# A two-layer diffusion backbone step on one core: the program records its instructions and orders each engine's queue itself, with the modulation products ranked last

## The chip, the core and the metric

The kernel runs on one core of one Trainium2 chip. Five engines of that core have a queue of their own and work through it strictly in order: TensorE (PE, matmuls; PEld are its weight loads), VectorE (DVE), ScalarE (ACT), GpSimd (POOL) and SyncE (SP), which here only issues the transfers from and to HBM. They meet through semaphores: an instruction that has to wait for another engine holds up all that is queued behind it on its own engine. The metric is the device time of one execution in microseconds (us), the median of several; lower is better. "Granted clock" is the share of TensorE's full clock that the chip granted in a stretch.

## The reference, cut to what matters

One inference step of a backbone of two layers, width 1024, on 128 context tokens and 512 latent tokens (640 columns in all), float32:

```
for each layer:
  shift, scale, gate (x2) = SiLU(cond) @ w_mod + b_mod      # cond = c (latent) or c_ctx (context)
  h = RMSNorm(x) * (1 + scale_a) + shift_a
  p = h @ w_in                                              # feeds all four mixers
  o_ssd = bidirectional Mamba-2 scan, 8 heads               # conv, softplus(dt), chunks of 128
  o_ret = bidirectional retention, 4 heads
  o_att = grouped-query attention, 8 heads, rotary
  o_mla = latent attention, 8 heads (two low-rank projections)
  g     = sigmoid(h @ w_merge + b_merge)                    # 1024 -> 4 x 1024
  x += gate_a * RMSNorm((sum_b g_b * (o_b @ w_br_b)) @ w_out)
  h = RMSNorm(x) * (1 + scale_f) + shift_f
  u = conv3(h @ w_ffn_up)                                   # 1024 -> 2 x 2816
  x += gate_f * RMSNorm((silu(u_gate) * u_up) @ w_ffn_down)
```

It returns both token groups and the final scan states and caches of the context.

## The kernel before

**Products.** Activations lie with features on the partitions, 640 columns of tokens. Each float32 operand is split in two parts, and each product is three matmuls: `wh*ah`, `wh*al`, `wl*ah`. Weights come as 128x512 blocks: SP loads `wr` (L333), ACT rounds it to `wh` (L305), POOL takes the difference `wl` (L308), and PE runs 128x128x320 matmuls over it (`mm`, L321; sums in `lin`). Activations come back through DVE and ACT: `tt` (L308), `stt` (L311), `tsc` (L316 and L318), `act` (L305). Other names in the rows: `st` and `pv` are PSUM tiles of scores, sums and attention values, `K` and `Q` keys, queries and conv inputs, `X` the residual or the accumulated merge, `g` gates, `ah` and `al` the two parts of the input of a product, `m` scratch, `la` the log decay of the scan.

**Stages.** `mixer` runs for each layer: `w_in` blocks with the SSD mixer, retention, attention, `merge` 0 to 2 (gates of a branch, its projection and the sum into `X`), the latent attention, and `merge_out` (merge 3, `w_out`, the two norms). `ffn` follows, with `up(f)` for 22 blocks and `down` in groups. The heavy products are dealt out between the heads of the mixers, so that PE has work while a chain of DVE and ACT works on a head.

**Modulation.** Layer 0's modulation is computed at the start on PE (`first`). Layer 1's, and the part of layer 0's that its second half needs, are computed while layer 0 runs (`mod_units`): a block of `w_mod` is loaded as 128x512, and DVE multiplies it with SiLU(cond) and sums along the row (L584, `wj<-K,silc` or `wj<-g,silc`, 320 of them, all in layer 0: each followed by a read of the accumulator). `fill(n)` takes n of them: 8 ahead of each of the 8 output blocks of a merge, 2 ahead of each block of merge 3, 5 after each `up(f)`, 2 ahead of each block of a `down`, and what is left with `fill(1000)`. Their weight tiles share the tags of the merge's `K` tiles (12) or of the FFN's `g` tiles (5).

**What sets the order.** The Tile framework orders each engine's queue, by the order in which the program is written and by hand-made edges: `tc.issue_after(x)` puts the instructions inside it behind x. `behind()` puts the matmuls of a head behind the PE instruction written last, `go_on` does so for the steps of the norms and scans that are dealt out between matmuls, `rowsum` and `first` for theirs, and `fill` puts the products behind `self.last`, the last DVE operation of an FFN block.

```
    def behind(self, on=True):
        return self.tc.issue_after(self.pe) if on else nullcontext()
```

## Time and profile before

| | |
|---|---|
| time, median of 3 runs | 3076.99 us (3075.81 to 3079.99) |
| the profiled execution | 3081.01 us, span of its trace 3079.2 us |
| busy: PE, PEld | 2911.7 us (95%), 2723.7 us (88%) |
| busy: DVE, ACT, POOL | 2019.1 us (66%), 1385.2 us (45%), 1148.1 us (37%) |
| granted clock of TensorE, mean | 0.975 |
| HBM traffic | 326.37 MB, 106 GB/s over the span |

Layer 0 runs from about 20 to 1586 us and layer 1 from there to the end. Busy time on PE is the time in which a matmul was in its pipeline; it says where PE stood still, not how well it was used. A timeline row gives the start, the length (of several in a row, from the first to the last), the engine, the line, the operation with output and inputs, the count and, in square brackets, the idle time ahead of it on its engine and what ended that. A windows row gives for one stretch (its bounds and its length) the busy time with the number of instructions of PE, PEld, DVE, ACT and POOL, then the granted clock, the share of the DMA engines and GB/s.

### The profile page before, as it was taken

The numbers are of one execution on the slowest core, as the hardware profiler recorded it, in microseconds if no ns is written. First come the engines' busy times: TensorE is split into PE (matmuls) and PEld (weight loads), VectorE is DVE, ScalarE is ACT, GpSimd is POOL, SyncE is SP. The second block draws the span as 40 slices with busy tenths as digits, with TensorE's granted clock in tenths as the row PEclk, the third lists the DMA queues.
The fourth block names the chain that finished last, engine by engine and source line by source line (L and its number), as shares of the span: only waits on it lengthen the run. The fifth ranks groups of instructions, "written<-read, shape, count | busy, mean of one in ns | idle before, by whom it ended". The sixth has DMA issues, their size and how long they took to land. (4 is left out here: it accounts for less than half of the span.)

```text
span 3079.2 us, 50917 instructions
## 1 busy us (share of the span) xinstructions
PE 2911.7 (95%) x18638; PEld 2723.7 (88%) x18638; DVE 2019.1 (66%) x3758; ACT 1385.2 (45%) x3013; POOL 1148.1 (37%) x889
## 2 busy tenths in 40 slices
PE   8999999999988899999988999999999999999998
PEld 4888898898888889899988899988988988999997
DVE  3678727637996588888776872177277455655556
ACT  3435246646634533332355353366477445433333
POOL 1223341131146653443463233411411566433334
PEclk9999999999999899999999999999999999999999
DMA  6215421143365434443243133211332433222223
GB/s 207 72 50 177 152 85 39 55 133 120 104 212 165 130 99 131 137 127 117 89 135 99 54 126 93 84 41 50 123 112 92 135 119 115 92 76 76 76 74 107
DMA packets 193418, 329.71 MB, mean 107 GB/s; under 512 B 20880, under 2 KB 54288, under 8 KB 193168
## 3 DMA queue, kind: packets, MB, share of 16 engines
q1 hardware_dynamic: 193168, 326.46, 34.1%
q8 instruction: 146, 2.39, 0.3%
q14 instruction: 104, 0.85, 0.1%
HBM read 293.41 MB, written 32.96 MB: 106 GB/s over the span
## 5 line engine op out<-in xcount | busy, mean ns | idle before, releaser
L308 POOL TENSOR_TENSOR wl<-wr,wh 128x512 fp32r<-128x512 f32 (+2 forms) x790 | 1076.5, 1366 | 1811.9 <-PE lin L321 1196.4
L321 PE MATMUL lin<-ah,wh 128*128 128x320 f32 (+1 forms) x3776 | 1173.4, 317 | 16.6 <-ACT ah L305 4.8
L321 PE MATMUL lin<-al,wh 128*128 128x320 f32 (+1 forms) x3776 | 1164.8, 315 | 12.5 <-DVE al L308 9.9
L321 PE MATMUL lin<-ah,wl 128*128 128x320 f32 x3744 | 949.2, 314 | 5.7 <-POOL wl L308 5.1
L305 ACT ACTIVATE wh<-wr 128x512 fp32r<-128x512 f32 (+2 forms) x796 | 486.7, 616 | 923.6 <-PE lin L321 491.7
L321 PEld LDWEIGHTS lin<-ah,wh 128*128 128x128 f32 (+1 forms) x3776 | 720.9, 191 | 32.6 <-ACT ah L305 6.6
L321 PEld LDWEIGHTS lin<-al,wh 128*128 128x128 f32 (+1 forms) x3776 | 719.8, 191 | 28.5 <-DVE al L308 13.8
L321 PEld LDWEIGHTS lin<-ah,wl 128*128 128x128 f32 x3744 | 656.5, 191 | 17.5 <-POOL wl L308 9.5
L308 DVE TENSOR_TENSOR m<-m,m 128x512 fp32r<-128x512 f32 (+6 forms) x393 | 310.1, 795 | 231.2 <-ACT m L305 225.5
L321 PE MATMUL lin<-K,wh 128*128 128x320 f32 (+1 forms) x1472 | 298.9, 316 | 16.6 <-ACT K L305 7.2
L305 ACT ACTIVATE m<-st 128x512 fp32r<-128x512 f32 (+2 forms) x480 | 223.3, 523 | 124.2 <-PE st L321 99.7
L321 PEld LDWEIGHTS lin<-K,wh 128*128 128x128 f32 x1472 | 240.7, 191 | 21.4 <-ACT K L305 7.8
L321 PE MATMUL lin<-O,wh 128*128 128x320 f32 x1024 | 215.7, 315 | 12.4 <-ACT O L305 4.6
L321 PE MATMUL lin<-K,wl 128*128 128x320 f32 (+1 forms) x736 | 187.5, 316 | 4.7 <-POOL wl L308 4.6
L321 PE MATMUL pv<-m,K 128*128 128x512 f32 (+2 forms) x832 | 184.1, 343 | 2.7 <-DVE m L308 2.5
L321 PEld LDWEIGHTS lin<-O,wh 128*128 128x128 f32 x1024 | 168.7, 191 | 18.6 <-DVE O L308 5.1
L584 DVE SCALAR_TENSOR_TENSOR wj<-g,silc 128x512 bf16<-128x512 f32 x160 | 148.1, 925 | 2.0
L584 DVE SCALAR_TENSOR_TENSOR wj<-K,silc 128x512 bf16<-128x512 f32 x160 | 139.3, 871 | 4.2 <-DMA K<-in_wmod 1.6
L321 PEld LDWEIGHTS pv<-m,K 128*64 128x64 f32 (+1 forms) x832 | 117.5, 160 | 27.1 <-DVE m L308 6.9
L305 ACT ACTIVATE m<-m 128x641 f32<-128x641 f32 (+4 forms) x116 | 82.4, 714 | 129.3 <-DVE m L311 120.5
L321 PEld LDWEIGHTS lin<-K,wl 128*128 128x128 f32 x736 | 129.6, 191 | 7.6 <-POOL wl L308 7.6
L1182 DVE TENSOR_REDUCE nm<-st 128x1 f32<-128x320 f32 (+1 forms) x288 | 123.9, 461 | 17.5 <-PE st L321 16.3
(209 smaller groups left out, 3360.6 us busy)
## 6 DMA issues: line engine op xcount, KB each, us to landing
wr<-in_wup SPq DMA_DIRECT2D x196, 256.0 KB, 2.7
wr<-in_wmg SPq DMA_DIRECT2D x160, 256.0 KB, 2.7
wr<-in_win SPq DMA_DIRECT2D x142, 256.0 KB, 2.6
K<-in_wmod SPq DMA_DIRECT2D x112, 256.0 KB, 3.9
wr<-in_wdn SPq DMA_DIRECT2D x94, 256.0 KB, 2.7
wr<-in_wbr SPq DMA_DIRECT2D x80, 256.0 KB, 2.7
g<-in_wmod SPq DMA_DIRECT2D x80, 256.0 KB, 2.9
wr<-in_wout SPq DMA_DIRECT2D x64, 256.0 KB, 2.8
```

The lines of the kernel that those rows point to most:

```text
L305: self.nc.scalar.activation(out, in_, func, **kw)
L308: return (eng or self.nc.vector).tensor_tensor(out, a, b, op).ins
L321: self.pe = self.nc.tensor.matmul(out, lhsT, rhs, start=start, stop=stop).ins
L584: self.nc.vector.scalar_tensor_tensor(junk[:, :512], w[:, :512], 0.5, si, ALU.mult, ALU.mult, accum_out=acc)
L1182: self.nc.vector.tensor_reduce(t[:, j * 8 + i : j * 8 + i + 1], p[:, :w], AX.X, ALU.max, negate=True)
```

## The change

The program no longer issues instructions while it is written. Every call goes to a `Recorder`, which notes the operation with the regions that it reads and writes. At the end `depend()` finds the dependences, `order()` plays all five queues against a table of durations, and `emit()` issues the instructions in the order of the starts so found, with the framework's own ordering switched off. In `order()` an engine that is free takes the operation with the lowest rank among those that could start; the rank is the place in the program, and an operation hands its rank on to what it needs. Buffers are part of it: an operation that needs a new tile can't start before one is free. `issue_after` becomes empty, so that none of the hand-made edges is left. The products of `mod_units` get a rank 4000 later (`BEHIND`), may not start before the last matmul written ahead of their `fill` (`gate`), and their weights get a tag of their own with 2 buffers (`wm`). The buffers of `g` go from 5 to 4 and those of `wh` from 4 to 3. The computation and the number of instructions on each engine stay the same.

```
-GB = 5
+GB = 4
-WR, WB, WL = 4, 4, 3
+WR, WB, WL = 4, 3, 3
+BEHIND = 4000
+LAT = {"tensor": 260.0, "vector": 90.0, "scalar": 90.0, "gpsimd": 110.0, "sync": 60.0}
+SLACK = 250.0
+DMA_ISSUE, DMA_NS, DMA_RATE = 400.0, 1900.0, 330.0
+class Recorder:
+    def add(self, eng, name, args, kw):
...
+        o.prio, o.gate = o.i + self.bias, self.gate
+    def cost(self, o):
...
+        if o.eng == "tensor":
...
+                return max(110.0, 10 + n * 0.428)
...
+        if o.eng == "vector":
+            if o.name == "reciprocal":
+                return 60 + 6.4 * n
+            if o.name in ("tensor_scalar", "memset"):
+                return 170 + 0.76 * n
+            if o.name == "scalar_tensor_tensor":
+                return 200 + 1.08 * n + (90 if "accum_out" in o.kw else 0)
+            return 180 + 1.06 * n
+        if o.eng == "scalar":
+            return 200 + 0.86 * n + (210 if "accum_out" in o.kw else 0)
+        if o.eng == "gpsimd":
...
+            return 260 + 2.12 * n
...
+    def depend(self):
...
+            if o.gate is not None:
+                o.preds.add(o.gate)
...
+        for o in reversed(self.ops):
+            for q in o.preds:
+                q.prio = min(q.prio, o.prio)
+    def order(self):
...
+            p, i = heappop(avail[e])
+            o = self.ops[i]
+            b = blocked(o, t) if o.new else None
...
+            for q in o.succs:
+                lat = 0.0 if q.eng == e and e != "sync" else LAT[e] + (SLACK if q.eng == "tensor" else 0.0)
+                q.ready = max(q.ready, o.end + lat)
...
+        done.sort(key=lambda o: o.start)
+    def emit(self):
+        done = self.order()
...
+        with self.tc.manual_schedule():
+            for o in done:
+                f = getattr(getattr(nc, o.eng), o.name)
+                f(*[_plain(v) for v in o.args], **{k: _plain(v) for k, v in o.kw.items()})
 class Net:
-        self.tc, self.nc, self.A = tc, tc.nc, A
+        self.rec = self.nc = Recorder(tc)
+    @staticmethod
+    def issue_after(ins):
+        return nullcontext()
     def mod_units(self, l, blocks, halves, tile, pool=()):
-                    w = self.modw(F32)
+                    self.rec.bias = BEHIND
+                    w = self.sbt(512, "wm", 2)
     def fill(self, n):
-        with self.tc.issue_after(self.last) if self.last is not None else nullcontext():
-            for _ in range(n):
+        self.rec.gate = self.pe
+        for _ in range(n):
...
+        self.rec.gate = None
 def build(tc, A, dbg=None):
-        Net(ctx, tc, A, dbg).run()
+        net = Net(ctx, tc, A, dbg)
+        net.run()
+        net.rec.emit()
-    with _tile.TileContext(nc, auto_bufs=True) as tc:
+    with _tile.TileContext(nc) as tc:
```

Three places show how instructions move. The first number of a row is its place in the engine's queue; a name carries the number that the program gave the tile, the same in both kernels, and a running number behind it. In the changed kernel the line is that of the recorder's call (L581).

VectorE at the end of merge 2 in layer 0, before: `X` takes the gated branch, `al` is the input of the `w_out` product made from it.

```order
1087 L308 TENSOR_TENSOR X_538_2794<-g_2457_10830,X_538_2794 128x320
1088 L584 SCALAR_TENSOR_TENSOR wj_2456_10828,modr_2154_9493<-K_2454_10824,silc_2176_9542 128x512
1089 L308 TENSOR_TENSOR X_539_2795<-g_2472_10896,X_539_2795 128x320
1090 L584 SCALAR_TENSOR_TENSOR wj_2470_10892,modr_2154_9493<-K_2469_10890,silc_2174_9537 128x512
1091 L584 SCALAR_TENSOR_TENSOR wj_2471_10894,modr_2154_9493<-K_2469_10890,silc_2176_9542 128x512
1092 L311 SCALAR_TENSOR_TENSOR g_2487_10962<-g_2487_10962,lin_2495_11001 128x320
1093 L584 SCALAR_TENSOR_TENSOR wj_2485_10958,modr_2154_9493<-K_2484_10956,silc_2174_9537 128x512
1094 L308 TENSOR_TENSOR X_540_2796<-g_2487_10962,X_540_2796 128x320
1095 L584 SCALAR_TENSOR_TENSOR wj_2486_10960,modr_2154_9493<-K_2484_10956,silc_2176_9542 128x512
1096 L308 TENSOR_TENSOR al0_26_98<-X_534_2790,ah0_18_90 128x320
```

And VectorE at the same place in the changed kernel:

```order
1063 L581 SCALAR_TENSOR_TENSOR g_2487_11007<-g_2487_11007,lin_2495_10994 128x320
1064 L581 TENSOR_TENSOR X_540_3975<-g_2487_11007,X_540_3975 128x320
1065 L581 TENSOR_TENSOR al0_26_294<-X_534_3051,ah0_18_290 128x320
1066 L581 TENSOR_TENSOR al1_27_307<-X_535_3271,ah1_19_301 128x320
1067 L581 TENSOR_TENSOR al2_28_322<-X_536_3471,ah2_20_318 128x320
1068 L581 TENSOR_TENSOR al3_29_343<-X_537_3606,ah3_21_331 128x320
1069 L581 TENSOR_TENSOR al4_30_354<-X_538_3727,ah4_22_351 128x320
1070 L581 TENSOR_TENSOR al5_31_375<-X_539_3851,ah5_23_361 128x320
1071 L581 TENSOR_TENSOR al6_32_412<-X_540_3975,ah6_24_404 128x320
1072 L581 SCALAR_TENSOR_TENSOR wj_2283_11085,modr_2154_10334<-wm_2282_10527,silc_2174_10285 128x512
1073 L581 SCALAR_TENSOR_TENSOR g_2502_11071<-g_2502_11071,lin_2510_11064 128x320
```

No product stands any more between `X_538` and `al6`; two stand around the last `X`, and the other products of this merge follow in a row behind `al7`.

TensorE at the first scores of attention in layer 1 (`K_4510` the keys, `Q_4519` the queries that DVE makes), before:

```order
11080 L321 MATMUL lin_4897_22677<-ah3_3589_16618,wl_4900_22680 128x320
11081 L321 MATMUL lin_4896_22676<-ah4_3590_16619,wh_4902_22709 128x320
11082 L321 MATMUL st_4522_21520<-K_4510_21476,Q_4519_21514 128x320
11083 L321 MATMUL st_4523_21523<-K_4510_21476,Q_4519_21514 128x320
11084 L321 MATMUL st_4524_21526<-K_4510_21476,Q_4519_21514 128x320
11085 L321 MATMUL lin_4896_22676<-al4_3598_16627,wh_4902_22709 128x320
```

In the changed kernel TensorE has at these scores:

```order
11121 L581 MATMUL lin_4896_21670<-ah7_3593_17415,wl_4903_21638 128x320
11122 L581 MATMUL lin_4897_21673<-ah7_3593_17415,wl_4903_21638 128x320
11123 L581 MATMUL lin_4905_21752<-O_4870_21297,wh_4908_21688 128x320
11124 L581 MATMUL st_4522_21756<-K_4510_20476,Q_4519_21727 128x320
11125 L581 MATMUL st_4523_21758<-K_4510_20476,Q_4519_21727 128x320
11126 L581 MATMUL st_4524_21760<-K_4510_20476,Q_4519_21727 128x320
```

The scores move behind the rest of the gate block `lin_4896`, `lin_4897` (4 of its 8 steps) and the first matmul of the next one: 24 matmuls more stand ahead of them.

VectorE at the start of the SSD scan in layer 1 (`m_3882` the softplus of dt on 128x80, 128x641 the convolution taps), before:

```order
1835 L311 SCALAR_TENSOR_TENSOR m_3909_18064<-K_3759_17325,hc_3583_16606,m_3909_18064 128x641
1836 L311 SCALAR_TENSOR_TENSOR m_3882_17964<-m_3882_17964 128x80
1837 L311 SCALAR_TENSOR_TENSOR g_4036_18578<-g_4036_18578,lin_4037_18579 128x320
1838 L311 SCALAR_TENSOR_TENSOR m_3882_17964<-m_3882_17964 128x80
1839 L311 SCALAR_TENSOR_TENSOR g_4036_18578<-g_4036_18578,lin_4038_18580 128x320
1840 L311 SCALAR_TENSOR_TENSOR dt_3881_17963<-m_3882_17964 128x80
1841 L318 TENSOR_SCALAR m_3912_18072<-K_3760_17326,hc_3583_16606 128x641
1842 L311 SCALAR_TENSOR_TENSOR la_3884_17984<-dt_3881_17963,ea_3883_17982 128x80
```

In the changed kernel VectorE has ahead of the same `la`:

```order
1803 L581 SCALAR_TENSOR_TENSOR O_3893_18049<-m_3894_18041,m_3892_18020 128x641
1804 L581 TENSOR_SCALAR m_3882_18047<-m_3882_18047 128x80
1805 L581 RECIPROCAL m_3882_18047<-m_3882_18047 128x80
1806 L581 TENSOR_TENSOR m_3882_18047<-m_3882_18047 128x80 x2
1807 L581 TENSOR_SCALAR m_3882_18047<-m_3882_18047 128x80
1808 L581 SCALAR_TENSOR_TENSOR m_3882_18047<-m_3882_18047 128x80 x8
1809 L581 TENSOR_SCALAR m_3882_18047<-dtx_3880_18043 128x80
1810 L581 SCALAR_TENSOR_TENSOR dt_3881_18111<-m_3882_18047 128x80
1811 L581 SCALAR_TENSOR_TENSOR la_3884_18115<-dt_3881_18111,ea_3883_16703 128x80
```

The convolution taps that stood between the steps of the softplus are gone from it, most of them to places ahead of it. On TensorE the cumulative sums that read `la` move from place 9175 to 9121 of the queue.

## Rows read from the trace of the kernel before

**Rows 1.** The page's first part: busy time, share of the span, instructions

```profile
PE 2911.7 (95%) x18638; PEld 2723.7 (88%) x18638; DVE 2019.1 (66%) x3758; ACT 1385.2 (45%) x3013; POOL 1148.1 (37%) x889
```

**Rows 2.** Windows (columns as told above): five stretches of layer 0, then of layer 1

```profile
135.60:466.80 331.20, 312.97 (x2098) 292.92 (x2097) 220.55 (x508) 128.41 (x298) 112.69 (x86) 0.99 0.36 112
474.50:681.00 206.50, 204.68 (x1272) 185.44 (x1272) 121.55 (x199) 119.42 (x255) 50.57 (x41) 1.00 0.22 68
681.00:883.30 202.30, 187.18 (x1113) 164.55 (x1111) 173.83 (x321) 121.56 (x252) 42.93 (x41) 0.98 0.44 139
883.30:1159.30 276.00, 240.83 (x1483) 232.14 (x1483) 201.96 (x361) 122.72 (x255) 158.93 (x113) 0.91 0.46 143
1159.30:1586.30 427.00, 408.51 (x2688) 400.16 (x2688) 360.67 (x673) 145.04 (x335) 184.66 (x133) 0.98 0.40 123
1694.40:2012.50 318.10, 309.42 (x2087) 289.40 (x2086) 161.62 (x375) 127.01 (x296) 109.89 (x86) 0.99 0.29 89
2020.20:2226.90 206.70, 204.62 (x1272) 185.40 (x1272) 120.12 (x198) 119.10 (x253) 52.49 (x41) 1.00 0.22 68
2226.90:2418.80 191.90, 185.28 (x1113) 164.49 (x1113) 135.33 (x216) 123.49 (x254) 44.16 (x42) 0.98 0.36 113
2418.80:2667.10 248.30, 230.13 (x1485) 224.40 (x1484) 149.64 (x232) 119.62 (x251) 149.71 (x114) 0.96 0.37 115
2667.10:3067.80 400.70, 395.32 (x2690) 393.93 (x2689) 217.89 (x353) 140.60 (x318) 162.30 (x130) 1.00 0.27 81
2700.00:2800.00 100.00, 100.00 (x684) 100.00 (x683) 54.32 (x88) 33.50 (x77) 37.62 (x29) 1.00 0.24 74
```

**Rows 3.** Windows of the tile wj alone: VectorE's busy time in the modulation products

```profile
135.60:466.80 331.20, 50.97 (x128) 0.99 0.36 112
...
681.00:883.30 202.30, 40.48 (x101) 0.98 0.44 139
883.30:1159.30 276.00, 62.82 (x122) 0.91 0.46 143
1159.30:1586.30 427.00, 135.76 (x290) 0.98 0.40 123
1694.40:3067.80 1373.40, 0.00 (x0) 0.99 0.30 91
```

**Rows 4.** The page's groups: busy, mean ns of one, of a modulation product

```profile
L584 DVE SCALAR_TENSOR_TENSOR wj<-g,silc 128x512 bf16<-128x512 f32 x160 | 148.1, 925 | 2.0
```

**Rows 5.** Timeline of VectorE at the end of merge 2, layer 0

```profile
1028.46 1.78 DVE L584 SCALAR_TENSOR_TENSOR wj<-K,silc 128x512 bf16<-128x512 f32 x1
...
1030.58 0.68 DVE L584 SCALAR_TENSOR_TENSOR wj<-K,silc 128x512 bf16<-128x512 f32 x1
...
1033.95 0.49 DVE L308 TENSOR_TENSOR al<-X,ah 128x320 fp32r<-128x320 f32 x1
```

**Rows 6.** Timeline of GpSimd at the same place

```profile
1021.14 8.56 POOL L308 TENSOR_TENSOR wl<-wr,wh 128x512 fp32r<-128x512 f32 x6 [2.65 <-ACT wh L305]
```

**Rows 7.** Timeline of TensorE at the same place

```profile
1034.49 0.64 PE L321 MATMUL lin<-al,wh 128*128 128x320 f32 x1 [4.85 <-DVE al L308]
```

**Rows 8.** Timeline of VectorE ahead of the first scores, attention, layer 1

```profile
2010.04 1.57 DVE L308 TENSOR_TENSOR X<-g,X 128x640 f32<-128x640 f32 x1
```

**Rows 9.** Timeline of TensorE at these scores

```profile
2012.51 0.71 PE L321 MATMUL st<-K,Q 128*128 128x320 f32 x3 [2.84 <-DVE Q L308]
```

**Rows 10.** Timeline of TensorE at the first scores of the latent attention, layer 1

```profile
2242.69 0.64 PE L321 MATMUL st<-K,Q 96*128 96x320 f32 x1 [1.83 <-ACT K L305]
```

**Rows 11.** Timeline of TensorE at the start of the SSD scan, layer 1

```profile
1670.45 0.90 PE L321 MATMUL st<-la,cst 128*128 128x40 f32 x6 [2.87 <-DVE la L311]
```

**Rows 12.** Timeline of VectorE ahead of that scan: waits for conv inputs

```profile
1640.46 0.16 DVE L318 TENSOR_SCALAR K<-lin 128x1 f32<-128x1 f32 x1 [3.36 <-PE lin L321]
```

**Rows 13.** Waits of the DMA queue on SP: us in total, times, longest

```profile
SPq L333 <- POOL wl L308: 1990.4, 674, 13.5
SPq L333 <- DVE wj L584: 223.1, 100, 8.0
```

More of the change, by code (lines that the diff above doesn't have):

```diff
@@ L228, with __init__, get @@
 KB = 12
-WR, WB, WL = 4, 4, 3
+WR, WB, WL = 4, 3, 3
 SEGS = ((0, 0, 128), (1, 128, 640))
+class Handle:
+    __slots__ = ("make", "real", "tag", "n", "first", "left", "end", "acc", "seq", "dram", "ro", "pe")
+    def __init__(self, make, n, tag=None, dram=False, ro=False):
+        self.make, self.real, self.tag, self.n = make, None, tag, n
+        self.left, self.end, self.acc, self.seq, self.dram, self.ro, self.pe = 0, 0.0, [], 0, dram, ro, None
+    def get(self):
+        if self.real is None:
+            self.real = self.make()
+        return self.real
@@ new lines, with _index, _rearrange @@
+_IX = {}
+def _index(shape):
+    if shape not in _IX:
+        n = 1
+        for v in shape:
+            n *= v
+        _IX[shape] = np.arange(n, dtype=np.int32).reshape(shape)
+    return _IX[shape]
+def _rearrange(ix, pattern, sizes):
+    left, right = (s.strip() for s in pattern.split("->"))
+    names, shape, k, group = [], [], 0, None
+    for tok in left.replace("(", " ( ").replace(")", " ) ").split():
+        if tok == "(":
+            group = []
+        elif tok == ")":
+            known = 1
+            for g in group:
+                known *= sizes.get(g, 1)
+            for g in group:
+                names.append(g)
+                shape.append(sizes.get(g, ix.shape[k] // known))
+            k += 1
+            group = None
+        elif group is not None:
+            group.append(tok)
+        else:
+            names.append(tok)
+            shape.append(ix.shape[k])
+            k += 1
+    return ix.reshape(shape).transpose([names.index(r) for r in right.split()])
@@ new lines, with __init__, shape, _with @@
+class View:
+    __slots__ = ("h", "ix", "ops", "dt")
+    def __init__(self, h, ix, ops, dt):
+        self.h, self.ix, self.ops, self.dt = h, ix, ops, dt
+    @property
+    def shape(self):
+        return list(self.ix.shape)
+    def _with(self, ix, name, *args, **kw):
+        return View(self.h, ix, self.ops + ((name, args, kw),), self.dt)
+    def __getitem__(self, s):
+        return self._with(self.ix[s], "__getitem__", s)
+    def rearrange(self, pattern, **sizes):
+        return self._with(_rearrange(self.ix, pattern, sizes), "rearrange", pattern, **sizes)
+    def unsqueeze(self, d):
+        return self._with(np.expand_dims(self.ix, d), "unsqueeze", d)
+    def to_broadcast(self, shape):
+        return self._with(np.broadcast_to(self.ix, shape), "to_broadcast", shape)
+    def bitcast(self, dt):
+        v = self._with(self.ix, "bitcast", dt)
+        v.dt = dt
+        return v
+    def make(self):
+        a = self.h.get()
+        for name, args, kw in self.ops:
+            a = getattr(a, name)(*args, **kw)
+        return a
+    def region(self):
+        a, b = int(self.ix.flat[0]), int(self.ix.flat[-1])
+        if self.h.dram:
+            return 0, 0, a, b
+        n = self.h.n
+        return a // n, b // n, a % n, b % n
@@ new lines, in _plain, with ins, __init__, __getattr__ @@
+def _plain(v):
+    return v.make() if isinstance(v, View) else v
+class Op:
+    __slots__ = ("i", "eng", "name", "args", "kw", "writes", "reads", "preds", "succs", "wait", "ready", "start", "end", "new", "tiles", "prio", "gate")
+    @property
+    def ins(self):
+        return self
+class Engine:
+    def __init__(self, rec, eng):
+        self.rec, self.eng = rec, eng
+    def __getattr__(self, name):
+        def call(*args, **kw):
+            return self.rec.add(self.eng, name, args, kw)
+        return call
@@ new lines, with __init__, tile @@
+class Pool:
+    def __init__(self, rec, pool, key):
+        self.rec, self.pool, self.key = rec, pool, key
+    def tile(self, shape, dt, tag, name, bufs=1):
+        rec, shape = self.rec, tuple(shape)
+        n = 1
+        for v in shape[1:]:
+            n *= v
+        tag_ = (self.key, tag)
+        h = Handle(lambda: self.pool.tile(list(shape), dt, tag=tag, bufs=bufs, name=name), n, tag_, self.key == "dr")
+        rec.bufs[tag_] = max(bufs, rec.bufs.get(tag_, 0))
+        h.seq = rec.count.get(tag_, 0)
+        rec.count[tag_] = h.seq + 1
+        return View(h, _index(shape), (), dt)
@@ L433, in rowsum @@
         p = self.pst()
-        with self.tc.issue_after(mm) if mm is not None else nullcontext():
+        with self.issue_after(mm) if mm is not None else nullcontext():
             for c in range(5):
@@ L503, in first @@
                 w = self.kt(F32)
-                with self.tc.issue_after(last) if last is not None else nullcontext():
+                with self.issue_after(last) if last is not None else nullcontext():
                     ins = self.load(w[:, :512], self.A["wmod0"][g, k])
-                with self.tc.issue_after(mm) if mm is not None else nullcontext():
+                with self.issue_after(mm) if mm is not None else nullcontext():
                     mm = self.mm(p[:2], s[:, 2 * k : 2 * k + 2], w[:, :512], k == 0, k == 7)
@@ L526, in first @@
                 for k in range(8):
-                    with self.tc.issue_after(last or ins):
+                    with self.issue_after(last or ins):
                         last = self.load(x[k][:, :T], self.A["x"][k])
@@ L658, in go_on @@
                 self.later.remove(e)
[L659 removed]
+                with self.issue_after(mm):
                     e[1]()
```

177 lines of the change are left out of this document (169 added, 8 removed).

## The prediction

> **What bounds the kernel now.** I read the page first. TensorE is busy 2911.7 of 3079.2 us [rows 1], so only some 170 us are open idleness. That share doesn't say how well it runs while it is busy, so the second view is the windows. In 2700 to 2800 us, in layer 1's FFN, TensorE never stands still and does 684 matmuls in 100 us [rows 2], 0.146 us each. That is the pace at which nothing can be won but by fewer matmuls, and the change removes none.
>
> The third view sets like against like. Both layers do the same work on TensorE, so I cut each into the same five stretches: the input products with SSD, retention and first merge; attention; second merges and latent attention; third merge and merge_out; FFN and its norm. The matmul counts agree within 11 in each [rows 2]. The lengths don't: 331.2 against 318.1 us (+13.1), 206.5 against 206.7 (-0.2), 202.3 against 191.9 (+10.4), 276.0 against 248.3 (+27.7), 427.0 against 400.7 (+26.3). Layer 0 takes 77.3 us more. What it has and layer 1 has not are the modulation products on VectorE, 50.97 + 40.48 + 62.82 + 135.76 = 290.0 us of them [rows 3], and the one stretch without products is the one without a difference. So the products, which feed nothing on TensorE until the layer's second half, cost 77 us by where they stand.
>
> Why, the timelines show. At the end of merge 2 six products stand ahead of `al`, one of 1.78 us and one of 0.68 us among those shown [rows 5], and TensorE stands still for 4.85 us until `al` is there [rows 7]. The long one ran while GpSimd made `wl` [rows 6], six of them in 8.56 us from 1021.14 on, so to 1029.70; the short one began after that. A product thus costs 0.7 or 1.8 us, by its neighbour.
>
> A second kind of loss is in both layers: hand-overs. At attention's first scores TensorE waits 2.84 us for `Q` [rows 9], and VectorE has just spent 1.57 us on `X` [rows 8], which nobody needs then. The latent attention's scores wait 1.83 us [rows 10].
>
> **The change, part by part.** No instruction is added or removed on any engine, so only waits can change. I sum against the profiled execution of 3081.0 us; it lies 4.0 above the median, so the same sum from the median is what I forecast.
>
> 1. *Products out of the chains.* The order of the changed kernel has none between `X` and `al` at merge 2's end but two, and two to four in the whole norm of merge_out. Their 290 us must still fit into VectorE's idle time: in layer 0's five stretches it is busy 220.55 + 121.55 + 173.83 + 201.96 + 360.67 = 1078.6 of 1443.0 us [rows 2], and now they may also fall into attention, where it is idle 85 us. I take, stretch by stretch, what I believe comes back. First: 10 of 13.1, since the products there go in runs of eight into merge 1, where VectorE waits for TensorE. Third: 4 of 10.4, as VectorE stays busy 86% of it. Fourth: 20 of 27.7, the place of the rows above. Fifth: 16 of 26.3, since after each `up` block products now stand singly, but VectorE is busy 84% of it. Sum: **-50 us**. Bounds: a third of 77, -25, and nearly all, -75.
>
> 2. *Hand-overs.* At attention's scores 24 more matmuls stand ahead on TensorE, 24 x 0.146 = 3.5 us, and `Q` now comes ahead of `X`; the wait of 2.84 goes in both layers. At the latent attention's scores the same holds for 1.83, also twice. Next late would be what `X` feeds, and that is used only a merge later. 2 x (2.84 + 1.83) = 9.3, taken as **-9 us** (bounds 0 and -12: smaller ones of the same kind).
>
> 3. *TensorE ahead of VectorE.* In the SSD stage the matmuls that read VectorE's results stand earlier: the sums over `la` by 54 places, 54 x 0.146 = 7.9 us. In the kernel before, VectorE waits there for conv inputs, 3.36 us at a time, four in a row alike [rows 12], and then `la` comes late, with 2.87 us of waiting [rows 11]. Now the taps of four convolutions fill these waits, and the softplus runs without them, so `la` is earlier by about as much: 0 here. In the SSD heads and the latent attention's heads TensorE's readers move up by 4 to 17 us, and VectorE by 1 to 8. Most of that was slack, but not all: I take **+8 us**, 2 for each stage and layer. Bounds: -6, the two waits at `la` gone, and +28, the 7 us by which the middle of the one lies ahead of the other, paid in full in two stages of two layers.
>
> 4. *The transfers.* Product weights now have two buffers and are loaded by SP in the same queue as `wr`. A load then waits for the product two tiles earlier, and all later `wr` loads stand behind it. SP waited for products already, 100 times and 223.1 us; it waited 674 times and 1990.4 us for `wl`, that is, because the buffers of `wr` were full [rows 13]. That is the cover: four blocks, each 24 matmuls or 3.5 us, less what `wh` loses with its fourth buffer; `g` loses one too, but the products that shared its buffers in the FFN no longer do. A product that is later than planned by up to some 10 us thus costs nothing; I take **0** (bounds 0 and +10, where the cover is gone at a few places).
>
> 5. *More waits.* TensorE's instructions carry 285 more semaphore waits. The 684 matmuls at 0.146 us show no price for one that is already met: **0** (bounds 0 and +6, 0.02 us each).
>
> Sum: -50 - 9 + 8 = **-51 us**, 3030 for the profiled execution and **3026** from the median of 3077.0.
>
> **The rivals.** *A: the table doesn't know the neighbour.* It gives a product 0.843 us; a row is 0.68 or 1.78 [rows 5], its mean 0.925 [rows 4], plus the read of the accumulator. VectorE then runs late against an order which fills its gaps exactly, and products ranked last still stand ahead of what the plan thought would come after. For it: GpSimd is busy 37% of the span, and in the third and fifth stretch VectorE is full to 84 and 86%. Against it: the product is one of many operations, and most are near the table. Then a third of 77 comes back, -25, the hand-overs half, -5, and the tight places cost 15: 3077 - 15 = **3062**. The Trainium skill, page "SBUF — State Buffer", section "Who interferes with whom", says that VectorE and GpSimd share a pair of ports as an exclusive lock, held for a whole instruction, and that the one that starts first decides who waits; it speaks against a plan that treats the two queues as free of each other. The trace agrees with it as far as a product of 1.78 us beside `wl` and of 0.68 us without it goes.
>
> *B, slower: TensorE's queue runs ahead of VectorE's.* TensorE's places are planned with VectorE on time. Where VectorE is nearly the bound, being late adds up over a stage, and TensorE, in order, waits at each reader with independent products queued behind it. The places are the first and third stretch of both layers, VectorE busy 220.55 + 173.83 + 161.62 + 135.33 = 691 us [rows 2]; if it runs a tenth longer than planned (0.925 against 0.843) and TensorE pays all of it, that is 69 us against 50 won and hand-overs that turn into such waits: 3077 + 19 = **3096**. It decides from the point at which TensorE pays more than 51 of the 69. For it: the readers were moved up more than VectorE's work. Against it: VectorE waits for TensorE there as well [rows 12], so that being late doesn't add up through a whole stage.
>
> *C: nearly all comes back.* Layer 0 becomes as fast as layer 1 (-75), hand-overs go (-12), nothing new waits: 3077 - 87 = **2990**. For it: attention's 85 us of idle VectorE; against it: the same order must then also be better in layer 1's chains.
>
> *D: no change.* What is won in layer 0 is lost at new waits in both: **3077**.
>
> **How the numbers follow.** Forecast case 0.50 (3005 to 3050), A 0.15 (3050 to 3075), B 0.17 (3083 to 3110), C 0.12 (2985 to 3005), D 0.06. A measurement of this kernel can tell about 0.2%, 6 us, from no change: 3071 to 3083 is "same". Faster: the forecast, C and 0.14 of A, 0.76; same: D and the rest of A, 0.07; slower: B, 0.17. The range is to hold 8 in 10: B stays out (0.17) and the lowest few of C, so 2990 to 3076.
>
> **What would show it right or wrong.** Right for 1: the windows of layer 0 come within 27 us of layer 1's stretch by stretch, with the wj rows now spread, some in attention, and the wait of 4.85 us at merge 2's end under 1. Right for 2: no wait over 0.5 us at the first scores of either attention. Step 3: waits of TensorE for VectorE in the SSD and latent-attention heads sum to under 10 us more than before; if layer 1's stretches, which have no products, are longer than 318.1 and 191.9 us, B is at work. Step 4: SP's waits for wj of over 10 us followed by a wait of TensorE for `wh`. Rival A shows as long products (1.8 us) right ahead of a VectorE result for which TensorE waits. The prediction is wrong if layer 1 changes by more than 15 us either way, since most of the sum is in layer 0.

## The result and the profile after

The changed kernel takes 3041.64 us (median of 4 runs, 3040.61 to 3048.55) against 3076.4 us (4 runs) for the kernel before. The ratio is 0.9892 with a 95% interval of 0.9873 to 0.9912, that is 33 us less, 27 to 39. Forecast were 51 less, 3026 us, in a range of 2990 to 3076. The direction and the range held; the amount is two thirds of what was forecast, and it came in part from other places than the ones I named, as the stretches below show.

The profiled execution of the changed kernel took 3048.55 us, 7 above its median. Its page, first part:

```profile
span 3046.8 us, 50154 instructions
## 1 busy us (share of the span) xinstructions
PE 2898.8 (95%) x18638; PEld 2710.4 (89%) x18638; DVE 2073.1 (68%) x3758; ACT 1387.8 (46%) x3013; POOL 1154.3 (38%) x889
```

TensorE's share reads as before [rows 1], and VectorE is busy 54 us longer. To see where the time went, I cut the execution at the places where TensorE had done the same amount of work as at the bounds of [rows 2]. The matmul counts of a stretch agree within 12 with those before, worth some 2 us at 0.146 us each. The windows of the changed kernel, in the order of [rows 2] (PE, PEld, DVE, ACT, POOL, clock, DMA), five of layer 0 and five of layer 1:

```profile
130.90:444.00 313.10, 308.13 (x2106) 290.90 (x2105) 202.01 (x483) 124.28 (x293) 108.02 (x86) 1.00 0.38 120
452.00:657.00 205.00, 204.85 (x1276) 185.56 (x1275) 130.60 (x210) 121.49 (x261) 54.35 (x43) 1.00 0.22 69
657.00:850.10 193.10, 187.07 (x1114) 165.48 (x1113) 153.75 (x249) 121.58 (x248) 43.01 (x41) 0.97 0.40 128
850.10:1126.80 276.70, 240.57 (x1486) 228.29 (x1485) 243.46 (x413) 120.37 (x254) 169.56 (x113) 0.95 0.46 147
1126.80:1551.30 424.50, 403.57 (x2690) 398.43 (x2690) 362.48 (x693) 145.40 (x331) 173.85 (x131) 0.98 0.42 128
1668.10:1982.30 314.20, 307.65 (x2098) 290.30 (x2098) 146.30 (x350) 122.98 (x290) 106.05 (x86) 1.00 0.29 91
1990.20:2195.70 205.50, 205.37 (x1278) 186.04 (x1277) 130.34 (x211) 121.08 (x259) 54.27 (x43) 1.00 0.23 71
2195.70:2388.10 192.40, 185.08 (x1115) 163.32 (x1114) 139.79 (x213) 121.42 (x248) 41.77 (x41) 0.99 0.35 110
2388.10:2628.40 240.30, 226.46 (x1483) 220.35 (x1481) 146.94 (x230) 120.31 (x251) 155.82 (x113) 0.98 0.38 119
2628.40:3034.40 406.00, 398.06 (x2690) 396.64 (x2688) 222.57 (x352) 143.83 (x319) 165.23 (x130) 0.99 0.26 80
```

| stretch | layer 0: before, after | layer 1: before, after |
|---|---|---|
| before the first stretch (set-up, or the FFN's norm and the start of SSD) | 135.6, 130.9 (-4.7) | 108.1, 116.8 (+8.7) |
| SSD, retention, merge 0 | 331.2, 313.1 (-18.1) | 318.1, 314.2 (-3.9) |
| attention | 206.5, 205.0 (-1.5) | 206.7, 205.5 (-1.2) |
| merge 1, latent attention | 202.3, 193.1 (-9.2) | 191.9, 192.4 (+0.5) |
| merge 2, merge_out | 276.0, 276.7 (+0.7) | 248.3, 240.3 (-8.0) |
| FFN and its norm | 427.0, 424.5 (-2.5) | 400.7, 406.0 (+5.3) |

The +5.3 at the bottom right belongs to this execution: in the kernel after_attn below, whose order in that stage is the same, it reads 400.5. So the gain is the first and the third stretch of layer 0 and layer 1's merge_out. Layer 1 as a whole, from 1551.3 us to the end, takes 1495.5 us against 1492.9 before. The fourth and fifth stretch of layer 0, where 36 of the 51 us were to come from, gave two.

The windows of the products alone, for the first, second, third and fourth stretch (this one in two parts), show what happened to them; an `x` counts a product and the read of its accumulator, so 128 rows are 64 products:

```profile
130.90:444.00 313.10, 55.63 (x128) 1.00 0.38 120
452.00:657.00 205.00, 0.00 (x0) 1.00 0.22 69
657.00:850.10 193.10, 15.26 (x34) 0.97 0.40 128
850.10:974.80 124.70, 67.63 (x118) 0.93 0.56 178
974.80:1126.80 152.00, 28.35 (x51) 0.97 0.38 122
```

Against [rows 3], 25 us of products have left the latent attention, and the fourth stretch has 96.0 instead of 62.8. None stands in attention. With the late rank they were put off as far as merge_out, which sums them.

The two waits of step 2 are gone or small. TensorE at the scores of [rows 9] and, in the second row, at those that follow [rows 10]:

```profile
1987.68 0.70 PE L581 MATMUL st<-K,Q 128*128 128x320 f32 x3 [0.77 <-DVE Q L581]
...
2211.61 2.21 PE L581 MATMUL st<-K,Q 96*128 96x320 f32 x6 [0.44 <-DVE nm L581]
```

### The profile page after: what moved, and what is told of

Same layout as the page of the kernel before. It is cut to its first block, busy times and chain, and to the rows that moved or that the text cites. A ratio compares the mean times of both kernels' runs of the same rounds, so it can differ in the third digit from the quotient of the medians.

```text
span 3046.8 us, 50154 instructions
## 1 busy us (share of the span) xinstructions
PE 2898.8 (95%) x18638; PEld 2710.4 (89%) x18638; DVE 2073.1 (68%) x3758; ACT 1387.8 (46%) x3013; POOL 1154.3 (38%) x889
## 5 line engine op out<-in xcount | busy, mean ns | idle before, releaser
L581 POOL TENSOR_TENSOR wl<-wr,wh 128x512 fp32r<-128x512 f32 (+2 forms) x790 | 1082.5, 1375 | 1734.4 <-ACT wh L581 1519.7
L581 PE MATMUL lin<-ah,wh 128*128 128x320 f32 (+1 forms) x3776 | 1170.5, 316 | 32.4 <-ACT K L581 11.7
L581 PE MATMUL lin<-al,wh 128*128 128x320 f32 (+1 forms) x3776 | 1158.6, 313 | 8.2 <-DVE al L581 8.0
L581 PE MATMUL lin<-ah,wl 128*128 128x320 f32 x3744 | 946.0, 313 | 14.3 <-POOL wl L581 14.2
L581 ACT ACTIVATE wh<-wr 128x512 fp32r<-128x512 f32 (+2 forms) x796 | 486.9, 616 | 915.2 <-PE lin L581 527.7
L581 PEld LDWEIGHTS lin<-ah,wh 128*128 128x128 f32 (+1 forms) x3776 | 715.8, 190 | 52.8 <-ACT wh L581 13.7
L581 PEld LDWEIGHTS lin<-al,wh 128*128 128x128 f32 (+1 forms) x3776 | 713.8, 189 | 23.0 <-DVE al L581 12.4
L581 PEld LDWEIGHTS lin<-ah,wl 128*128 128x128 f32 x3744 | 651.3, 189 | 32.6 <-POOL wl L581 22.4
L581 DVE TENSOR_TENSOR m<-m,m 128x512 fp32r<-128x512 f32 (+6 forms) x393 | 313.4, 804 | 156.9 <-ACT m L581 151.4
L581 DVE SCALAR_TENSOR_TENSOR wj<-wm,silc 128x512 bf16<-128x512 f32 x320 | 310.6, 970 | 55.9 <-DMA wm<-in_wmod 50.9
L581 PE MATMUL lin<-K,wh 128*128 128x320 f32 (+1 forms) x1472 | 299.0, 316 | 19.5 <-DVE O L581 10.0
L581 ACT ACTIVATE m<-st 128x512 fp32r<-128x512 f32 (+2 forms) x480 | 220.4, 522 | 144.6 <-PE st L581 122.8
L581 PEld LDWEIGHTS lin<-K,wh 128*128 128x128 f32 x1472 | 241.1, 192 | 23.4 <-ACT Q L581 9.1
L581 PE MATMUL lin<-O,wh 128*128 128x320 f32 x1024 | 215.5, 314 | 2.9 <-DVE g L581 1.4
L581 PE MATMUL pv<-m,K 128*128 128x512 f32 (+2 forms) x832 | 205.9, 343 | 4.5 <-DVE m L581 4.3
L581 PE MATMUL lin<-K,wl 128*128 128x320 f32 (+1 forms) x736 | 187.4, 315 | 3.0 <-POOL wl L581 2.9
L581 PEld LDWEIGHTS lin<-O,wh 128*128 128x128 f32 x1024 | 167.5, 189 | 8.9 <-DVE O L581 2.1
L581 DVE TENSOR_REDUCE nm<-st 128x1 f32<-128x320 f32 (+1 forms) x288 | 124.8, 462 | 37.0 <-PE st L581 35.0
L581 PEld LDWEIGHTS pv<-m,K 128*64 128x64 f32 (+1 forms) x832 | 116.8, 160 | 20.6 <-DVE m L581 7.6
L581 PEld LDWEIGHTS lin<-K,wl 128*128 128x128 f32 x736 | 130.2, 192 | 3.8 <-POOL wl L581 3.7
L581 PE MATMUL st<-Q,K 128*128 128x512 f32 (+3 forms) x480 | 133.5, 380 | 0.0
L581 PE MATMUL lin<-O,wl 128*128 128x320 f32 x512 | 130.1, 312 | 2.2 <-POOL wl L581 2.2
```

Of the source, the lines that this page charges most:

```text
L581: f(*[_plain(v) for v in o.args], **{k: _plain(v) for k, v in o.kw.items()})
```

## The experiments

Twelve kernels, each timed against the kernel before; ratios come with their 95% interval. All but before_narrow and before_bufs are edits of the changed kernel.

**What products cost at all: after_narrow and before_narrow.**

```
-  scalar_tensor_tensor(junk[:, :512], w[:, :512], 0.5, si, ..., accum_out=acc)
+  scalar_tensor_tensor(junk[:, :2], w[:, :2], 0.5, si[:, :2], ..., accum_out=acc)
```

> The changed kernel, but each modulation product takes 2 columns of its weight block instead of 512, so that VectorE has nearly nothing to do for it; the loads, the count and the places of the instructions stay (the modulation of layer 1 is then not the reference's). Theory P (what layer 0 still loses against layer 1 in merge 2, merge_out and the FFN, 36 + 19 us in the trace of the changed kernel, is the products): about 3041 - 50 = 2990 us, and the two layers' stretches become alike within 8 us. Rival O (the products cost little any more where they now stand, the rest is the order of everything else): 3030 us or more.

> The kernel before with the same 2-column products; the framework then orders the other instructions somewhat differently too. Theory P (the difference of 77 us between the layers was the products): about 3077 - 75 = 3002 us. What lies between this and the changed kernel with narrow products is what the recorded order does for everything else: about 12 us by P. Rival O: 3050 us or more, as layer 0 would be longer for other reasons, and the new order would be worth 30 us without any product.

Measured: after_narrow 3010.31 us, 0.9783 (0.9769 to 0.9798); before_narrow 3016.4 us, 0.9801 (0.9786 to 0.9815). The products cost the kernel before 1.99% or 61 us, and the changed kernel 1.09% or 34 us (0.9892 - 0.9783), good to some 5 and 8 us by the intervals. Neither theory had the size: P's 75 and 50 were too much, O's 10 too little. And without products the new order is worth 6 us in sum, not 12 to 30, and the two intervals overlap. (A narrow product still takes 0.29 us in the mean, so both numbers are a little low. The plan, too, is made with the shorter product, 0.29 instead of 0.84 us: 568 of VectorE's operations and 74 of TensorE's stand elsewhere than in the changed kernel, so, against what I expected, not all places stay.)

Cut at equal numbers of matmuls, the two narrow kernels also tell in which stretch the products cost. Layer 0's first, third, fourth and fifth stretch in before_narrow and then in after_narrow:

```profile
137.00:460.30 323.30, 311.37 (x2097) 291.67 (x2097) 178.86 (x507) 127.95 (x298) 109.61 (x86) 0.99 0.36 115
674.40:874.30 199.90, 187.69 (x1113) 165.42 (x1112) 148.21 (x356) 122.26 (x253) 41.88 (x42) 0.97 0.48 157
874.30:1124.10 249.80, 230.44 (x1485) 224.71 (x1484) 159.53 (x327) 121.91 (x253) 149.54 (x113) 0.96 0.45 144
1124.10:1525.30 401.20, 395.71 (x2689) 393.41 (x2687) 278.36 (x672) 146.09 (x335) 167.96 (x134) 1.00 0.42 131
```

```profile
132.20:445.20 313.00, 307.24 (x2098) 289.98 (x2097) 160.77 (x477) 124.19 (x292) 106.24 (x86) 1.00 0.38 120
659.70:850.80 191.10, 184.69 (x1114) 162.52 (x1112) 148.34 (x262) 121.72 (x248) 41.77 (x41) 0.99 0.41 134
850.80:1104.10 253.30, 231.47 (x1485) 223.39 (x1484) 177.02 (x408) 121.32 (x254) 154.65 (x113) 0.97 0.50 160
1104.10:1515.20 411.10, 400.97 (x2689) 399.34 (x2688) 261.45 (x683) 147.47 (x331) 168.11 (x131) 0.98 0.42 131
```

| stretch of layer 0 | products cost before | products cost after | the new order without products |
|---|---|---|---|
| SSD, retention, merge 0 | 331.2 - 323.3 = 7.9 | 313.1 - 313.0 = 0.1 | 313.0 - 323.3 = -10.3 |
| merge 1, latent attention | 202.3 - 199.9 = 2.4 | 193.1 - 191.1 = 2.0 | 191.1 - 199.9 = -8.8 |
| merge 2, merge_out | 276.0 - 249.8 = 26.2 | 276.7 - 253.3 = 23.4 | 253.3 - 249.8 = +3.5 |
| FFN and its norm | 427.0 - 401.2 = 25.8 | 424.5 - 411.1 = 13.4 | 411.1 - 401.2 = +9.9 |

So the 6 us of the new order are a small rest of large terms of both signs: it wins 10 and 9 us in the mixers' first and third stretch, and loses 10 in layer 0's FFN and 9 at layer 1's start (the table of the result). Each number is from one execution of a kernel, so a difference of 2 or 3 us says nothing.

**The rank alone: after_rank0.**

```
-BEHIND = 4000
+BEHIND = 0
```

> The changed kernel with the products ranked by their place in the program (4000 set to 0). Only 568 of VectorE's rows and 329 of TensorE's stand elsewhere. Theory R (the late rank keeps products out of the chains and brings most of the gain): 3065 us or more. Rival G (the gaps of VectorE are found by the table of durations, and the rank hardly matters): within 8 us of the changed kernel, 3034 to 3050 us.

Measured: 3072.69 us (10 runs), 0.9984 (0.9975 to 0.9993). Theory R holds: the late rank carries 28 us, though it moves few rows. By equal work, the kernel is as fast as the changed one up to the middle of merge_out and then loses at merge_out's norm and in the FFN. The stretch at that norm where the changed kernel takes 28.5 us (DVE 28.36, clock 1.00) reads here:

```profile
969.40:1013.20 43.80, 30.02 (x166) 28.46 (x165) 38.51 (x85) 18.12 (x42) 20.54 (x15) 0.82 0.36 114
```

with 12.92 us of products in it; the granted clock of the stretch is 0.82.

**No gate: after_nogate.**

```
-        self.rec.gate = self.pe
+        self.rec.gate = None
-                    cb = self.m() if pool else self.g()
+                    cb = self.m() if pool else self.sbt(512, "wm", 2)
```

> The changed kernel without the gate that keeps a product behind the last matmul ahead of its fill, and with the tile that the cond vector is loaded into taken from the products' own tag, so that products can run as early as their two buffers allow: some 70 of 320 now stand in attention, where VectorE idles, and none in the second half of the FFN. Theory P: of the 55 us that layer 0 still takes more than layer 1, 25 to 40 go, so 3002 to 3017 us. Rival O: no change, 3036 to 3046 us. Rival S (their loads stand early in SP's queue and hold up the weights' loads): slower than 3046 us, with waits of SP for wj of more than 10 us.

Measured: 3039.24 us, 0.9877 (0.986 to 0.9893), no difference to the changed kernel. Theory P fails as I had put it. By equal work the FFN is some 19 us shorter, but 8 us are lost in the set-up, and layer 1's products move up into merge 2 and merge_out, where the first part still holds 64 us of them:

```profile
865.00:983.00 118.00, 64.14 (x108) 0.95 0.56 177
```

SP's longest wait for a product is 9.8 us, so rival S doesn't show. I read from it that what counts is not how early a product may start but which place it fills.

**Products out of the place ahead of the norm: after_attn; out of the FFN too: after_layer1.** after_attn writes what is left of layer 0's products ahead of attention. after_layer1 does so in both layers and takes 128 of layer 1's products into layer 1.

```
+        if l == 0:            # after_layer1: without the condition
+            self.fill(1000)
         r = self.att_in(l, hh, hl)
...                            # after_layer1 only:
-            self.filler = self.mod_units(1, range(48), ...)
+            self.filler = self.mod_units(1, range(16), ...)
...
             hh, hl = self.ffn(l, x, Gf, hh, hl)
+            if l == 0:
+                self.filler = self.mod_units(1, range(16, 48), ...)
```

> The changed kernel, with the 64 products of layer 0 that merge 2 dealt out written ahead of attention instead, so that they may run in attention's idle time of VectorE; those of layer 1 stay. Theory D (merge_out's norm needs the last of layer 0's products; ranked last they pile up in merge 2 and ahead of that norm, where VectorE is busy 49 of 54 us and 8 to 10 us are lost): 3041 - 9 = 3032 us, with no loss at the norm. Rival F (it is VectorE's fullness in that place whatever fills it, and layer 1's products move up into it): 3038 to 3044 us.

> As after_attn, and 128 of layer 1's products (blocks 16 to 47, which only layer 1's merge_out needs) are dealt out in layer 1's merge 0 and attention instead of in layer 0's merge 3 and FFN. Theory P (a product costs where VectorE is full, 14 us of the FFN's 18, and nothing in merge 0 and attention): 3032 - 8 = 3024 us, with layer 1's first two stretches no more than 3 us longer. Rival M (a product costs about 0.1 us wherever it stands): 3032 to 3041 us.

Measured: after_attn 3017.14 us, 0.981 (0.979 to 0.983); after_layer1 2999.64 us, 0.9754 (0.9736 to 0.9772), faster than either kernel of the change. Theories D and P hold in kind; the gains, 25 and 17 us, are two to three times what they gave. Windows of after_attn, the first and fourth stretch of layer 0 and the last of layer 1, and then its products in the first and in the two parts of merge 2 and the norm that follows:

```profile
130.50:446.70 316.20, 308.91 (x2105) 290.79 (x2104) 240.90 (x568) 124.91 (x295) 111.86 (x86) 1.00 0.43 139
851.70:1097.20 245.50, 228.92 (x1485) 222.18 (x1485) 198.78 (x305) 121.81 (x254) 162.27 (x113) 0.97 0.43 139
2602.60:3003.10 400.50, 394.92 (x2690) 393.54 (x2688) 222.71 (x350) 142.38 (x317) 162.33 (x129) 1.00 0.25 81
```

```profile
130.50:446.70 316.20, 93.22 (x208) 1.00 0.43 139
851.70:904.20 52.50, 23.60 (x32) 1.00 0.57 185
904.20:949.50 45.30, 2.50 (x6) 0.97 0.46 149
```

Forty of the 64 now stand in the first stretch (104 products instead of 64) and make it 3 us longer, the other 24 in attention; with the 64 out of it, the fourth is 31 us shorter than the changed kernel's 276.7. In after_layer1, the FFN of layer 0 and, in layer 1, the first stretch with 104 products in it read:

```profile
1097.20:1504.70 407.50, 399.55 (x2691) 398.45 (x2690) 250.13 (x423) 145.22 (x326) 169.17 (x131) 0.98 0.29 90
1621.60:1934.70 313.10, 307.30 (x2099) 289.99 (x2099) 242.31 (x567) 125.00 (x294) 116.55 (x86) 1.00 0.43 140
```

The FFN gets 15 us shorter than after_attn's 422.4, and layer 1's first stretch isn't longer than without any product (314.2 in the changed kernel).

**Whether anything is left: layer1_narrow**, after_layer1 with the edit of after_narrow.

> after_layer1 with products of 2 columns. Theory P (products are nearly free where they stand now): within 8 us of 2999.6, so 2992 to 2999 us. Rival M (they still cost about 0.1 us each, 30 us): 2970 us.

Measured: 3004.56 us, 0.977 (0.9747 to 0.9792), the interval of after_layer1 overlaps. Theory P holds: where they now stand, 320 products cost nothing that can be measured. The plan is made anew here too, and more than 1600 of TensorE's rows change, so a cost of some us could hide behind another order.

**The hand-made edges: after_edges.**

```
-    @staticmethod
-    def issue_after(ins):
-        return nullcontext()
+    @contextmanager
+    def issue_after(self, ins):
+        old, self.rec.gate = self.rec.gate, ins
+        yield
+        self.rec.gate = old
```

> The changed kernel with the hand-made edges kept, as dependences in the recorded order (an operation inside one may not start before the instruction that it names). Theory H (what layer 1 loses at its start, 9 us from the FFN's norm to the SSD heads, comes from the edges that are gone): about 10 us less, 3031 us, in both layers. Rival T (it comes from TensorE's places planned ahead of VectorE by the table): 3036 to 3046 us with the same waits at the softplus's input.

Measured: 3052.98 us, 0.9925 (0.9904 to 0.9946), some 10 us slower than the changed kernel, though the two intervals overlap a little. Theory H falls: layer 1 loses as much at its start as without edges. Rival T's waits are there, but its time is missed. One place where the edges cost is the set-up; the stretch up to the first bound, 130.9 us in the changed kernel, is here

```profile
0.00:141.20 141.20, 119.30 (x652) 85.61 (x653) 78.56 (x158) 57.90 (x121) 29.62 (x28) 0.95 0.41 139
```

This execution is the shortest of the four, and as a whole as long as the changed kernel's profiled one (spans 3045.9 and 3046.8 us), so it doesn't show where the difference of the medians lies.

**The plan told of the shared port: after_lock.**

```
+            if e in ("vector", "gpsimd") and <two inputs in SBUF>:
+                c += max(0.0, port.get(<the other>, 0.0) - t)
+                port[e] = t + c
```

> The changed kernel whose plan makes an operation of VectorE with two inputs in SBUF wait for a tensor_tensor of GpSimd that is under way, and the other way round. Theory A (the order goes wrong where the plan knows nothing of the neighbour: 75 of 320 products take 1.5 us or more): 15 us less, 3026 us, with fewer long products. Rival G (the waits come from a product that has begun when the chain's operation becomes ready, not from its length): 3036 to 3046 us, or more, since products now also stand in layer 1.

Measured: 3110.14 us, 1.0112 (1.0089 to 1.0134), 68 us slower than the changed kernel. Theory A's remedy fails. The fuller plan puts 46 products off into layer 1, and TensorE waits longer; its longest waits:

```profile
PE st L585 <- DVE m L585: 39.4, 17, 7.3
PE lin L585 <- ACT g L585: 25.6, 2, 23.9
```

One wait alone holds 23.9 us. That long products don't matter isn't shown by it; that a plan with this cost is better is refuted.

**TensorE ahead of VectorE: layer1_slack and layer1_dve**, on after_layer1.

```
-SLACK = 250.0
+SLACK = 1000.0                                              # layer1_slack
-            c = self.cost(o)
+            c = self.cost(o) * (1.12 if e == "vector" else 1.0)   # layer1_dve
```

> after_layer1 with the time that the plan keeps between another engine's result and a TensorE instruction that needs it raised from 250 to 1000 ns; 5632 of TensorE's rows move by a median of 0 and at most 240 places. Theory B (TensorE stands ahead of a late VectorE, which costs 8 us at the start of layer 1's SSD and some at the start of the FFN): 2999.6 - 10 = 2990 us, with the 12 us that the start of layer 1 loses there down to 4. Rival V (it is VectorE's own order there, the convolution taps ahead of the softplus, and TensorE's place doesn't matter): 2996 to 3004 us.

> after_layer1 with all durations of VectorE in the plan 12% longer, about what the trace shows in the mean (2246 us summed against 1976 of the table). Theory B' (VectorE runs late against its plan, and TensorE's queue stands wrong by what it is late): 2990 us or less; the sums over la go back to the place that they had in the kernel before. Rival V: 2996 to 3004 us. Rival L (as with the modelled port, a fuller plan puts products off to layer 1's last stages): slower than 3004 us.

Measured: 3017.13 us, 0.9815 (0.9797 to 0.9833), and 3022.08 us, 0.9835 (0.9812 to 0.9857), 18 and 22 us slower than after_layer1. Theories B and B' fall. By equal numbers of matmuls layer 1 loses with the slack 3 us more at its start than after_layer1; with the longer durations it gets 5 us back there and loses 14 in the SSD heads that follow. Why a plan nearer to the measured mean gives a worse order is open.

**The buffers: before_bufs.**

```
-GB = 5
+GB = 4
-WR, WB, WL = 4, 4, 3
+WR, WB, WL = 4, 3, 3
```

> The kernel before with the changed kernel's buffers, 4 of g and 3 of wh, and nothing else. Step 4 of the prediction (the buffers that go cost nothing): within 6 us of the kernel before, 3071 to 3083 us. Rival W (the product weights, which share g in the FFN there, are loaded later): 3085 us or more.

Measured: 3072.18 us (10 runs), 0.9993 (0.9983 to 1.0003). Step 4's price of nothing holds for the buffers.

## Why the prediction was right or wrong

**The whole: a good number, in part by luck.** Of the -51, the products were to give -50 and the order of everything else -1; they gave -27 and -6. But that -6 is the rest of terms of some 10 us, most of which stand in no step of the sum, and which nearly cancel.

**Step 1, products: right in kind, wrong by half and wrong in place.** The forecast was -50; the products went from 61 to 34 us, -27. The base of 77 us, the difference of the layers, was too large: before_narrow gives the products 26 us each in the fourth and fifth stretch, as I had, but 8 of 13.1 in the first and 2 of 10.4 in the third, where layer 0 stays longer without their work. The term that failed is "Fourth: 20 of 27.7": their cost there went from 26 to 23. "Fifth: 16 of 26.3" came as 12, but the new order takes 10 of them back. In the first stretch 8 came where 10 were forecast, in the third nothing where 4 were; what else these two stretches got shorter by, 10 and 9 us, is the order's. And attention, where I thought that products might now fall, has none: merge 0's are done before it, and `gate` keeps merge 2's behind a matmul that comes after it.

I read in the order that the products had left the chain at merge 2's end, and it is so: the wait for `al` of [rows 7] is gone, and the longest one left there is

```profile
1001.39 0.41 PE L581 MATMUL lin<-ah,wl 128*128 128x320 f32 x1 [1.44 <-POOL wl L581]
```

But I didn't ask where they went. An operation hands its rank on to what it needs, and layer 0's modulation is summed at the head of `merge_out`; so the last 64 products of layer 0 have the rank of these sums, ahead of merge 3 and its norm, whatever `BEHIND` says, and the late rank could only move them up to there: 67.63 us of products in 124.7 us, against 40.36 in the 122.5 us of the same work before:

```profile
883.30:1005.80 122.50, 40.36 (x76) 0.89 0.56 175
```

Of the 59 products there 47 are layer 0's. The other 12 are the first ones of layer 1, which come behind its new `silc`. Their rank is truly last, and the order has them in the gaps that the table leaves between the norm's squares `m`, for 0.84 us each. VectorE ahead of the first sums of that norm, and TensorE's wait for them (the first and the last product of a run; between them stand five more and two squares):

```profile
931.41 1.28 DVE L581 SCALAR_TENSOR_TENSOR silc<-silc,g 128x512 f32<-128x512 f32 x2
...
936.51 1.65 DVE L581 SCALAR_TENSOR_TENSOR wj<-wm,silc 128x512 bf16<-128x512 f32 x1
...
947.49 0.69 DVE L581 SCALAR_TENSOR_TENSOR wj<-wm,silc 128x512 bf16<-128x512 f32 x1
...
948.10 0.48 DVE L581 TENSOR_TENSOR m<-m,m 128x320 f32<-128x320 f32 x1
```

```profile
948.64 1.44 PE L581 MATMUL st<-cst,m 128*128 128x1 f32 x6 [2.74 <-DVE m L581]
```

Products that take 1.65 us here, right ahead of a result for which TensorE waits, are rival A's sign. after_attn shows what layer 0's products cost in this stretch by taking them away: 31 us; after_narrow, which only makes all of them short, gives 23.

The late rank is what makes the change a gain at all: without it the recorded order is at 0.9984.

**Step 2, hand-overs: right in the main.** 2.84 became 0.77, and the 1.83 of [rows 10] 0.44, in layer 1, and layer 0 is alike (2.85 to 0.78, 1.82 to 0.44). 9 us were forecast, 6.9 are gone by these rows, less a new wait of 0.68 us for `g` just ahead of the first scores in each layer. The sign that I set, no wait over 0.5 us, is missed by the 0.77.

**Step 3, TensorE ahead of VectorE: wrong in place, and for the SSD heads in sign.** I gave the start of SSD 0 and the heads 8 in all. In layer 1, where no product stands, the stretch of the SSD heads got 3.9 us shorter (318.1, 314.2), that of the latent attention 0.5 longer, and the start lost 8.7. The wait at `la` fell from 2.87 [rows 11] to 0.98 as expected, but a new one stands ahead of it, at the softplus's input, since VectorE now does convolution taps first. The longest new wait of this start stands earlier still, 4.90 us for ScalarE's `K`. TensorE at the two and at `la`, and VectorE's last operations ahead of the softplus:

```profile
1585.34 0.64 PE L581 MATMUL lin<-ah,wh 128*128 128x320 f32 x1 [4.90 <-ACT K L581]
...
1624.14 0.35 PE L581 MATMUL st<-cst,m 16*128 16x16 f32 x3 [3.40 <-DVE m L581]
...
1634.72 0.90 PE L581 MATMUL st<-la,cst 128*128 128x40 f32 x6 [0.98 <-DVE la L581]
```

```profile
1622.03 0.61 DVE L581 TENSOR_SCALAR m<-K,hc 128x641 f32<-128x641 f32 x1
1622.67 0.89 DVE L581 SCALAR_TENSOR_TENSOR m<-K,hc,m 128x641 f32<-128x641 f32 x1
1623.59 0.49 DVE L581 TENSOR_TENSOR m<-m,lin 48x320 f32<-48x320 f32 x1
```

That the taps are the cause of the 3.40 is read from the rows; slack, edges and longer durations didn't cure it. The 4.90 is gone in layer1_dve, whose start is 5 us shorter; it is in the changed kernel, after_layer1 and after_edges alike, and halved (2.4) with the slack.

**Steps 4 and 5: right.** SP waited for products 110 times and 176.8 us, at most 5.4, against [rows 13]; before_bufs is level. In layer 1's FFN, without products, the stretch is 400.5 us in after_attn against 400.7 before, so waits that are already met show no price there.

**Not in the sum:** the set-up became 4.7 us shorter, and 10 us longer again in after_edges; what the new order costs in layer 0's FFN and its norm, 10 us without the products' work, is open; and in layer 1's merge_out, without any product, 8.0 us went. There the view of waits (us in total, times, longest) has TensorE's waits of matmuls into `st`, the norms' sums, for VectorE's `m`, before and after; they make up 5.5 of the 8.0:

```profile
PE st L321 <- DVE m L308: 7.9, 2, 5.6
```

```profile
PE st L581 <- DVE m L581: 2.4, 1, 2.4
```

**The rivals.** A's mechanism is real: products of 1.5 us and more rose from 55 to 75, the sum of all products from 287.4 to 310.6 us, and the rows above show one place where it delays a norm. What it costs in all is not shown, since the plan that was told of the neighbour made things worse. B didn't happen beyond the 8.7 us. C's 2990 wasn't reached by the change, but after_layer1 comes within 10 us of it.

## What to carry to other kernels

Filler work costs by the place that it fills, not by its amount or by how early it may start: 320 products, 286 to 311 us of VectorE, cost 61, 34 or nothing measurable. A late rank holds only until an operation with an early rank needs the result, so ask first which operation that is and where it is written, and put the filler into a stage with an idle engine well ahead of it. Compare stretch by stretch and with the filler made short: a sum that comes out nearly right can be made of larger terms that cancel. When an order says what has left a chain, find out where it now stands before a gain is booked. A more careful table of durations isn't by itself a better order.

## What the runs showed of the hardware

In after_narrow a product of 2 columns takes 0.16 us in the median, and up to 1.28 us beside GpSimd's `wl`. VectorE and GpSimd at one such place:

```profile
830.50 1.14 DVE L581 SCALAR_TENSOR_TENSOR wj<-wm,silc 128x2 bf16<-128x2 f32 x1 [1.71 <-DMA wm<-in_wmod]
...
831.68 0.16 DVE L581 SCALAR_TENSOR_TENSOR wj<-wm,silc 128x2 bf16<-128x2 f32 x1
```

```profile
830.33 1.30 POOL L581 TENSOR_TENSOR wl<-wr,wh 128x512 fp32r<-128x512 f32 x1 [2.21 <-ACT wh L581]
```

The product ends at 831.64 and the `wl` at 831.63: it lasted until GpSimd's instruction was over, whatever its own length. So did all 46 products of this run that took over 0.5 us: each ends within 0.03 us of the end of a `wl`. The Trainium skill, page "SBUF — State Buffer", section "Who interferes with whom", says that a VectorE instruction with two inputs in SBUF contends with a GpSimd instruction that reads SBUF; the row agrees, with inputs of 2 columns.
